# A fifth Strassen pair in two gate branches of a hybrid decoder layer, and norm weights applied per channel

## Chip, cores, metric

The kernel runs on one core of a Trainium2 chip. The time is device time in microseconds (us) of one execution of the program. Engines are called as in the profile: PE is the matrix engine (PEld its weight loads), DVE is VectorE, ACT is ScalarE, POOL is GpSimd, SP is the engine that issues most DMAs.

## The reference, cut to what matters

One decoder layer over 256 positions of 2048 channels. One input projection feeds three mixers (a gated linear recurrence, a windowed attention, a short convolution); each is projected back to 2048 channels, weighed by a sigmoid gate computed from the input, and the sum goes through one output projection and a layer norm.

```python
u = x @ w_in[l]                                   # 2048 -> 16896, all float32
...
o_a = o_a * lax.rsqrt(jnp.mean(jnp.square(o_a), axis=-1, keepdims=True) + RMS_EPS)
o_a = o_a.reshape(bsz, t, HGRN_WIDTH) * hgrn_norm_g[l].astype(jnp.float32)
y_a = (o_a.astype(x.dtype) * jax.nn.silu(a_g)) @ w_proj_hgrn[l]
y_b = (o_b * jax.nn.silu(b_g)) @ w_proj_attn[l]
y_c = (o_c * jax.nn.silu(c_g)) @ w_proj_conv[l]
merged = jax.nn.sigmoid(m_a) * y_a + jax.nn.sigmoid(m_b) * y_b + jax.nn.sigmoid(m_c) * y_c
y = merged @ w_out[l]
x = layer_norm(ALPHA * x + y, ln_g[l], ln_b[l])
```

## The kernel before

Every float32 product is made of three matmuls on two-part numbers: a weight block is split into `hi` (rounded, made by ACT, line 114) and `lo` (the rest, made by DVE, line 115), x likewise, and PE adds x-hi times `hi`, x-lo times `hi` and x-hi times `lo`. Weights come in loads of 1 MB into three `raw` buffers; `hi` and `lo` have four buffers each. `w8` is a pool of twelve 8 KB tiles (`t8`) that everything long-lived shares; `w4` holds smaller tiles of the mixers and is closed before the gates begin, and `mgp` then takes its memory.

First come the input projections, with the mixers cut into small steps (`tasks`) that `pump` strews between the projections' loads; the last of the input projections is the convolution `conv(3)`, whose results are added up by ACT copies `rest` and DVE (lines 191, 192, 541). `sums_of_x`, one of these tasks, loads x again and makes the sums of blocks that the Strassen scheme needs.

Then, for each branch (a, b, c) and each half of the gate's columns, `pair_of_groups` computes 256 rows by 1024 columns of gate from 2048 input channels, and two `gemm` calls do the branch's projection. That makes six gate calls, call 0 (branch a) to call 5 (branch c). A seventh call computes half of the output projection (`w_out2`). Each call goes through eight *pairs of rows*: a pair is 256 input channels, two blocks of 128. A plain pair multiplies 2 x 2 blocks of x with 2 x 2 blocks of weights in 8 products of 3 matmuls. A pair marked in `PAIRS` uses Strassen's scheme in Winograd's form: 7 products, of sums of x (made beforehand) and sums of weights. For these DVE makes four weight sums `w` (lines 696 to 698) out of `raw`, and `w` is split into `hw` (ACT, 2048 columns) and `lw` (DVE); of `raw` itself only three blocks out of four are split. `hw` and `lw` lie in `mgp`, one buffer each, or, for every second marked pair, in `w8`, as far as `spare` says. Marked are pairs 1, 3, 5 and 7.

The eight sums of products gather in eight PSUM banks. `p1`, `p2`, `p6`, `p7` are of the pool `accp`, which the projections use too, so `p6` and `p7` take the banks of the projection just before; `p5`, `p3`, `p4`, `px` are of the pool `bgp`. After a projection DVE evacuates its two banks (lines 749 and 750; line 752 in branch a; 767 with the statistics of line 770 in the output projection).

In which order the products of a marked pair are written is chosen in this line (`whole` needs only `hi` and `lo`, `summed` needs `hw` and `lw`, of `rest` one needs `hi2` and one `hw`):

```python
for n, y in enumerate(whole + summed + rest if raw_first or end else summed + rest[::-1] + whole):
    product(*y, end)
```

The order written in the code is not the order on the engines: a planner sorts each engine's instructions by its own estimate of when operands and buffers are ready, among those ready by the order of writing, and each engine then works through its queue in that fixed order.

The norm weights of branch a (`gn`, 1024 values spread to all partitions) are multiplied into the gate by POOL (line 592); the recurrence's last step transposes its output and splits it with `split_to` (lines 87, 88).

Of the kernel before, what the change touches and what calls it, by code (L numbers as in the profile page):

```python
# [16 lines left out]
P = 128  # L17
T = 256
# [26 lines left out]
PAIRS = (0, 1, 0, 1, 0, 1, 0, 1)  # L45
# [5 lines left out]
def hybrid_kernel(ctx, tc, a, out):  # L51
# [15 lines left out]
    def t8(shape, name, dt=F32):  # L67
        return w8.tile(shape, dt, tag="w8", name=name)
# [131 lines left out]
    def constants():  # L200
# [15 lines left out]
        c["gn"] = const.tile([P, HW], F32, name="gn")  # L216
        nc.sync.dma_start(out=c["gn"], in_=a["hgrn_norm_g"].partition_broadcast(P))
# [67 lines left out]
    def hgrn(hf, fk, q, v, gate):  # L285
# [148 lines left out]
        for i, ps in transpose_pairs([[o[:, t, h * P : h * P + P] for t in range(2)] for h in range(4)], "oaT"):  # L434
            split_to(outs["a"][hf][:, i : i + 2], ps)
            yield
# [112 lines left out]
    def sums_of_x():  # L549

        n = len(pairs)
        xr = rawp.tile([P, n, 2, T], F32, tag="raw", name="xr")
        for i, p in enumerate(pairs):
            nc.sync.dma_start(out=xr[:, i], in_=a["xT"][:, 2 * p : 2 * p + 2])
        sx = t8([P, 4, n, P], "sx")
        block_sums([sx[:, j] for j in range(4)], xr[:, :, 0, :P], xr[:, :, 1, :P], xr[:, :, 0, P:], xr[:, :, 1, P:])
        yield
        for i in range(0, n, 2):
            dst = t8([P, 2, 4, 2, P], "sums", F32R)
            sums.append(dst)  # L560
            for j in range(2):
                split_to(dst[:, j], sx[:, :, i + j])
            yield
# [13 lines left out]
    for hf in range(2):  # L577
# [53 lines left out]
    pairs = [p for p in range(KT // 2) if PAIRS[p]]  # L631
    sums = []
# [10 lines left out]
    msums = []  # L643

    def turn(m, d):
        dst = t8([P, 4, 2, T], "m", F32R)
        ms.append(dst)
        if d % 2 == 0:
            msums.append(t8([P, 2, 4, 2, P], "msums", F32R))
        for i, ps in transpose_pairs([[m[:, t, c * P : c * P + P] for t in range(2)] for c in range(4)], "mT"):  # L650
            split_to(dst[:, i : i + 2], ps)
            if PAIRS[2 * d + i // 2]:
# [4 lines left out]
                split_to(msums[d // 2][:, d % 2], sx)  # L657
            yield

    def pair_of_groups(src, x, sums, raw_first, spare):  # L660
# [18 lines left out]
        final = max(p for p in range(KT // 2) if not PAIRS[p])  # L679
        for p in range(KT // 2):  # L680
# [3 lines left out]
            if not PAIRS[p]:  # L684
# [18 lines left out]
            i = pairs.index(p)  # L703
# [3 lines left out]
            sx = [[sums[i // 2][:, i % 2, j, m] for m in range(2)] for j in range(4)]  # L707
# [214 lines left out]
```

## Time and profile before

| | us |
|---|---|
| median of three runs | 1003.6 (1002.97 to 1003.93) |
| the profiled execution | 1002.37 |
| its span, first to last instruction | 1000.5 |
| PE busy | 984.0 |
| DVE busy | 797.5 |
| ACT busy | 562.3 |
| POOL busy | 32.4 |

A share of busy time is an average over all stages. Matmuls are listed longer than the distance of their starts, since they are pipelined. Times in rows are from the span's start.

### The profile page before, as it was taken

What the parts mean: (1) busy time and instruction counts of PE and PEld (TensorE: products, weight loads), DVE (VectorE), ACT (ScalarE), POOL (GpSimd) and SP (SyncE); (2) the same over time, 40 slices, a digit from 0 to 9 for tenths busy, and PEclk for the clock granted to TensorE, in tenths of its full rate; (3) what the DMA queues carried; (4) which work ended last, traced back from release to release, by engine and by line L of the source; (5) the groups of instructions that cost most, each with busy time, mean ns of one, the idle gap of its engine ahead of it and who ended that gap; (6) DMA issues with size and microseconds to landing.
All of it is one profiled execution on the core that took longest, in us unless ns stands there. A gap on an engine that the chain in (4) does not pass through costs nothing.

```text
span 1000.5 us, 13721 instructions
## 1 busy us (share of the span) xinstructions
PE 984.0 (98%) x5430; PEld 828.5 (83%) x5430; DVE 797.5 (80%) x1000; ACT 562.3 (56%) x735; POOL 32.4 (3%) x32
## 2 busy tenths in 40 slices
PE   8999999999999999999999999999999999999995
PEld 5888888888888888888888888888888888888884
DVE  6557889689955666767778898887989889897997
ACT  5545668557564655645655555555555555564551
POOL 1000100220010000000000000000000000000003
PEclk9999999999999999999999999999999999999998
DMA  8755545444455445544555655555645556548542
GB/s 318 261 174 205 176 161 172 166 171 168 171 179 200 174 163 187 192 169 165 185 197 177 229 190 205 209 210 196 214 180 209 211 193 215 182 171 338 206 168 84
DMA packets 30831, 193.67 MB, mean 194 GB/s; under 512 B 3840, under 2 KB 4640, under 8 KB 8752
## 3 DMA queue, kind: packets, MB, share of 16 engines
q1 hardware_dynamic: 28944, 185.90, 52.4%
q10 hardware_dynamic: 1152, 4.72, 1.2%
q0 software_dynamic: 672, 2.20, 0.7%
q8 instruction: 42, 0.69, 0.3%
q14 instruction: 21, 0.17, 0.0%
HBM read 190.68 MB, written 2.12 MB: 193 GB/s over the span
## 4 chain that ended last, share of the span: by engine, by line
PE 96%; DVE 2%; DMA 1%; SPq 0%; issue 0%; ACT 0%
PE acc L151 25%; PE acc L150 12%; PE p L671 9%; PE p L673 9%; PE p L672 9%; PE acc L145 9%; PE acc L143 9%; PE acc L144 8%; DMA raw<-in_w_rows 1%; PE sc L464 1%; PE acc L153 1%; PE pvb L506 1%; DVE xres L793 1%; DVE xres L791 1%; PE pT L497 1%; PE lev L390 0%
## 5 line engine op out<-in xcount | busy, mean ns | idle before, releaser
L114 ACT CAST hi<-raw 128x1024 fp32r<-128x1024 f32 (+1 forms) x341 | 343.9, 1013 | 317.1 <-PE p L672 107.9
L115 DVE TENSOR_TENSOR lo<-raw,hi 128x1024 fp32r<-128x1024 f32 (+1 forms) x341 | 397.0, 1175 | 111.4 <-ACT hi L114 109.5
L151 PE MATMUL acc<-xs,hi 128*128 128x512 f32 x1056 | 372.0, 397 | 0.0
L150 PE MATMUL acc<-xs,lo 128*128 128x256 f32 x990 | 279.0, 282 | 0.0
L151 PEld LDWEIGHTS acc<-xs,hi 128*128 128x128 f32 x1056 | 197.3, 188 | 44.4 <-issue 1.2
L150 PEld LDWEIGHTS acc<-xs,lo 128*128 128x128 f32 x990 | 186.9, 189 | 3.7 <-issue 1.2
L671 PE MATMUL p<-hi,xs 128*128 128x512 f32 x240 | 93.5, 390 | 0.0
L673 PE MATMUL p<-lo,xs 128*128 128x512 f32 x240 | 93.5, 389 | 0.0
L672 PE MATMUL p<-hi,xs 128*128 128x512 f32 x240 | 93.5, 389 | 0.0
L115 DVE TENSOR_TENSOR lw<-w,hw 128x2048 fp32r<-128x2048 f32 x28 | 64.2, 2293 | 22.3 <-ACT hw L114 20.9
L143 PE MATMUL acc<-hi,xs 128*128 128x512 f32 (+1 forms) x160 | 60.2, 376 | 2.3 <-ACT hi L114 2.3
L145 PE MATMUL acc<-lo,xs 128*128 128x512 f32 (+1 forms) x160 | 59.0, 371 | 0.3 <-DVE lo L115 0.3
L144 PE MATMUL acc<-hi,xs 128*128 128x512 f32 (+1 forms) x160 | 59.0, 369 | 0.0
L114 ACT CAST hw<-w 128x2048 fp32r<-128x2048 f32 x28 | 53.6, 1913 | 9.6 <-DVE w L698 9.5
L673 PEld LDWEIGHTS p<-lo,xs 128*128 128x128 f32 x240 | 45.1, 188 | 9.4
L672 PEld LDWEIGHTS p<-hi,xs 128*128 128x128 f32 x240 | 45.1, 188 | 9.3
L671 PEld LDWEIGHTS p<-hi,xs 128*128 128x128 f32 x240 | 45.1, 188 | 9.3
L191 ACT COPY rest<-acc 128x256 f32<-128x256 f32 x66 | 24.0, 372 | 42.1 <-PE acc L151 41.4
L143 PEld LDWEIGHTS acc<-hi,xs 128*128 128x128 f32 x160 | 30.2, 189 | 10.0 <-ACT hi L114 4.7
L145 PEld LDWEIGHTS acc<-lo,xs 128*128 128x128 f32 x160 | 30.1, 189 | 6.6 <-DVE lo L115 1.6
L696 DVE TENSOR_TENSOR w<-raw 128x1024 f32<-128x1024 f32 x28 | 34.2, 1220 | 0.9 <-DMA raw<-in_w_gate 0.7
L144 PEld LDWEIGHTS acc<-hi,xs 128*128 128x128 f32 x160 | 30.2, 189 | 4.7
(261 smaller groups left out, 1458.6 us busy)
## 6 DMA issues: line engine op xcount, KB each, us to landing
raw<-in_w_cols SPq DMA_DIRECT2D x68, 1024.0 KB, 4.8
raw<-in_w_gate SPq DMA_DIRECT2D x48, 1024.0 KB, 4.8
raw<-in_w_out SPq DMA_DIRECT2D x16, 1024.0 KB, 4.8
raw<-in_w_rows SPq DMA_DIRECT2D x12, 1024.0 KB, 4.8
raw<-in_w_proj_hgrn SPq DMA_DIRECT2D x8, 1024.0 KB, 4.8
raw<-in_w_proj_attn SPq DMA_DIRECT2D x8, 1024.0 KB, 4.8
raw<-in_w_proj_conv SPq DMA_DIRECT2D x8, 1024.0 KB, 4.8
raw<-in_w_rows SPq DMA_DIRECT2D x7, 512.0 KB, 8.7
```

Source lines behind the costliest of these rows:

```text
L114: nc.scalar.copy(out=hi, in_=r)
L115: nc.vector.tensor_sub(out=lo, in0=r, in1=f32(hi))
L143: nc.tensor.matmul(out=acc, lhsT=xk[:, 0, ts], rhs=hi, start=first, stop=False)
L144: nc.tensor.matmul(out=acc, lhsT=xk[:, 1, ts], rhs=hi, start=False, stop=False)
L145: nc.tensor.matmul(out=acc, lhsT=xk[:, 0, ts], rhs=lo, start=False, stop=last)
L150: nc.tensor.matmul(out=acc[:, :T], lhsT=lo, rhs=xk[:, 0], start=False, stop=False)
L151: nc.tensor.matmul(out=acc, lhsT=hi, rhs=xk, start=first, stop=last)
L191: nc.scalar.copy(out=rest[p], in_=acc[p, T:])
L671: nc.tensor.matmul(out=ps, lhsT=x[0], rhs=hi, start=begins, stop=False)
L672: nc.tensor.matmul(out=ps, lhsT=x[1], rhs=hi, start=False, stop=False)
L673: nc.tensor.matmul(out=ps, lhsT=x[0], rhs=lo, start=False, stop=last)
L696: nc.vector.tensor_sub(out=w[:, 0:2], in0=raw[:, 0:1].to_broadcast([P, 2, NC]), in1=raw[:, 1::2])
```

## The change

The marked pairs become 0, 2, 3, 5 and 7 in branches b and c (calls 2 to 5), and 0, 2, 5 and 7 in branch a and in `w_out2`. Pair 0 is thus a Strassen pair in every call. For pair 0, and for all but the last in branch a and `w_out2`, products are written as `rest`, `summed` in reverse, `whole`. The block sums of x are made in three lots (two pairs, two pairs, one pair), their raw sums in `w4`, and the fifth pair's split sums have a tile of their own, `fifth`. `gn` shrinks to one value per channel and partition, and is applied where branch a's output is split after its transposition; the POOL product goes.

```diff
-PAIRS = (0, 1, 0, 1, 0, 1, 0, 1)
+PAIRS, FEWER = (0, 2, 3, 5, 7), (0, 2, 5, 7)
...
-        c["gn"] = const.tile([P, HW], F32, name="gn")
-        nc.sync.dma_start(out=c["gn"], in_=a["hgrn_norm_g"].partition_broadcast(P))
+        c["gn"] = const.tile([P, 8], F32, name="gn")
+        nc.sync.dma_start(out=c["gn"], in_=a["hgrn_norm_g"])
...
-            split_to(outs["a"][hf][:, i : i + 2], ps)
+            for j in range(2):
+                g = C["gn"][:, 4 * hf + i + j : 4 * hf + i + j + 1]
+                dst = outs["a"][hf][:, i + j]
+                nc.scalar.mul(out=dst[:, 0], in_=ps[:, j], mul=g)
+                nc.vector.scalar_tensor_tensor(out=dst[:, 1], in0=ps[:, j], scalar=g, in1=f32(dst[:, 0]),
+                                               op0=ALU.mult, op1=ALU.subtract)
...
-        n = len(pairs)
-        xr = rawp.tile([P, n, 2, T], F32, tag="raw", name="xr")
-        for i, p in enumerate(pairs):
-            nc.sync.dma_start(out=xr[:, i], in_=a["xT"][:, 2 * p : 2 * p + 2])
-        sx = t8([P, 4, n, P], "sx")
-        block_sums([sx[:, j] for j in range(4)], xr[:, :, 0, :P], xr[:, :, 1, :P], xr[:, :, 0, P:], xr[:, :, 1, P:])
-        yield
-        for i in range(0, n, 2):
-            dst = t8([P, 2, 4, 2, P], "sums", F32R)
-            sums.append(dst)
-            for j in range(2):
-                split_to(dst[:, j], sx[:, :, i + j])
+        fifth = const.tile([P, 4, 2, P], F32R, name="fifth")
+        for at in range(0, len(PAIRS), 2):
+            ps = (FEWER + tuple(p for p in PAIRS if p not in FEWER))[at : at + 2]
+            n = len(ps)
+            xr = rawp.tile([P, n, 2, T], F32, tag="raw", name="xr")
+            for i, p in enumerate(ps):
+                nc.sync.dma_start(out=xr[:, i], in_=a["xT"][:, 2 * p : 2 * p + 2])
+            sx = t4([P, 4, n, P], "sx")
+            block_sums([sx[:, j] for j in range(4)], xr[:, :, 0, :P], xr[:, :, 1, :P], xr[:, :, 0, P:], xr[:, :, 1, P:])
+            yield
+            dst = t8([P, n, 4, 2, P], "sums", F32R) if n == 2 else None
+            for i, p in enumerate(ps):
+                sums[p] = dst[:, i] if n == 2 else fifth
+                split_to(sums[p], sx[:, :, i])
             yield
...
-        nc.gpsimd.tensor_mul(out=gate, in0=gate,
-                             in1=C["gn"][:, hf * NC : hf * NC + NC].rearrange("p (o n) -> p o n", o=1)
-                             .to_broadcast([P, 2, NC]))
...
-            for n, y in enumerate(whole + summed + rest if raw_first or end else summed + rest[::-1] + whole):
+            for n, y in enumerate(whole + summed + rest if p and (raw_first or end) else rest + summed[::-1] + whole):
...
-            sg = pair_of_groups(a["w_gate"][2 * n + half], xs, sums, n > 0, 2 if n else 1)
+            sg = pair_of_groups(a["w_gate"][2 * n + half], xs, sums, PAIRS if n else FEWER, n > 0, 2 if n else 1)
...
-    y = pair_of_groups(a["w_out2"][0], ms, msums, False, 0)
+    y = pair_of_groups(a["w_out2"][0], ms, msums, FEWER, False, 0)
```

`turn` makes the sums of the merged rows for the pairs in `FEWER` in the same way as before for the pairs in `PAIRS`.

## Rows read from the trace of the kernel before

**Rows 1.** The page's first section: busy time, share of the span, instructions.

```profile
PE 984.0 (98%) x5430; PEld 828.5 (83%) x5430; DVE 797.5 (80%) x1000; ACT 562.3 (56%) x735; POOL 32.4 (3%) x32
```

**Rows 2.** Waits of PE: engine, line, waited for: us in total, times, longest.

```profile
PE acc L143 <- ACT hi L114: 2.3, 2, 1.3
...
PE acc L145 <- DVE l L115: 0.7, 1, 0.7
PE acc L145 <- DVE lo L115: 0.3, 1, 0.3
```

**Rows 3.** Timeline of PE in call 0: start, duration (us), what [idle before].

```profile
523.22 0.39 PE L671 MATMUL p<-hi,xs 128*128 128x512 f32 x1
...
528.66 0.39 PE L671 MATMUL p<-hw,sums 128*128 128x512 f32 x1
528.89 0.39 PE L672 MATMUL p<-hw,sums 128*128 128x512 f32 x1
529.12 0.39 PE L671 MATMUL p<-hw,sums 128*128 128x512 f32 x1
529.34 0.39 PE L672 MATMUL p<-hw,sums 128*128 128x512 f32 x1
529.57 0.39 PE L671 MATMUL p<-hw,sums 128*128 128x512 f32 x1
529.81 0.73 PE L673 MATMUL p<-lw,sums 128*128 128x512 f32 x2
```

**Rows 4.** Lines by shape, whole run: busy us, mean ns | idle before, releaser.

```profile
L115 DVE TENSOR_TENSOR lo<-raw,hi 128x1024 fp32r<-128x1024 f32 x311 | 378.0, 1222 | 108.4 <-ACT hi L114 106.7
L115 DVE TENSOR_TENSOR lw<-w,hw 128x2048 fp32r<-128x2048 f32 x28 | 64.2, 2293 | 22.3 <-ACT hw L114 20.9 <-PE p L673 1.4
L114 ACT CAST hw<-w 128x2048 fp32r<-128x2048 f32 x28 | 53.6, 1913 | 9.6 <-DVE w L698 9.5
L696 DVE TENSOR_TENSOR w<-raw 128x1024 f32<-128x1024 f32 x28 | 34.2, 1220 | 0.9 <-DMA raw<-in_w_gate 0.7
L698 DVE TENSOR_TENSOR w<-raw,w 128x512 f32<-128x512 f32 x28 | 19.3, 688 | 0.4
```

**Rows 5.** Busy time of each engine in one gate call with its projections (call 3).

```profile
core 0: us, PE busy (x) PEld busy (x) DVE busy (x) ACT busy (x) POOL busy (x), PEclk, DMA share, GB/s
711.00:773.60 62.60, 62.60 (x277) 51.86 (x277) 56.35 (x59) 35.10 (x33) 0.00 (x0) 1.00 0.57 202
```

**Rows 6.** Lines in calls 1 to 5 (586 to 877 us), DVE, then ACT by shape.

```profile
L115 DVE TENSOR_TENSOR lo<-raw,hi 128x1024 fp32r<-128x1024 f32 x113 | 125.8, 1127 | 19.2 <-ACT hi L114 18.4
...
L114 ACT CAST hi<-raw 128x1024 fp32r<-128x1024 f32 x93 | 97.9, 1053 | 111.8 <-PE p L672 72.3 <-PE acc L144 27.3 <-issue 11.0
```

**Rows 7.** Timeline of ACT and DVE around call 0, then DVE before call 4.

```profile
523.07 0.78 ACT L191 COPY rest<-acc 128x256 f32<-128x256 f32 x2 [1.38 <-PE acc L151]
...
524.27 1.92 ACT L114 CAST hw<-w 128x2048 fp32r<-128x2048 f32 x1
...
527.47 2.28 DVE L115 TENSOR_TENSOR lw<-w,hw 128x2048 fp32r<-128x2048 f32 x1
...
771.53 2.29 DVE L115 TENSOR_TENSOR lw<-w,hw 128x2048 fp32r<-128x2048 f32 x1 [0.85 <-ACT hw L114]
```

**Rows 8.** Timeline around the start of the `w_out2` call: ACT, PE, DVE.

```profile
918.30 2.00 ACT L114 CAST hi<-raw 128x1024 fp32r<-128x1024 f32 x2 [2.58 <-DMA raw<-in_w_out]
...
924.40 0.39 PE L671 MATMUL p<-hi,m 128*128 128x512 f32 x1
...
925.46 0.68 DVE L767 SCALAR_TENSOR_TENSOR xres<-xres,acc 128x512 f32<-128x512 f32 x1
...
928.60 0.75 DVE L770 BATCH_NORM_STATS2 stats<-xres 128x6 f32<-128x256 f32 x2
929.26 0.67 DVE L767 SCALAR_TENSOR_TENSOR xres<-xres,acc 128x512 f32<-128x512 f32 x1
```

**Rows 9.** Norm weights on POOL, and the nearest 128x256 form on DVE.

```profile
L592 POOL TENSOR_TENSOR ga<-ga,gn 128x1024 f32<-128x1024 f32 x2 | 6.6, 3318 | 99.8 <-DVE ga L197 99.8
...
L530 DVE SCALAR_TENSOR_TENSOR yc<-hp,cw,yc 128x256 f32<-128x256 f32 x16 | 6.7, 478 | 0.0
```

More of the change, by code (lines that the diff above doesn't have):

```diff
@@ L630, in hybrid_kernel @@
         tasks.append(attn(hf, q, kz, vb, gate))
-    pairs = [p for p in range(KT // 2) if PAIRS[p]]
-    sums = []
+    sums = {}
     tasks.append(sums_of_x())
@@ L641, in hybrid_kernel @@
     ms = []
-    msums = []
+    msums, dsts = {}, []
     def turn(m, d):
@@ L647, in turn @@
         ms.append(dst)
-        if d % 2 == 0:
-            msums.append(t8([P, 2, 4, 2, P], "msums", F32R))
         for i, ps in transpose_pairs([[m[:, t, c * P : c * P + P] for t in range(2)] for c in range(4)], "mT"):
             split_to(dst[:, i : i + 2], ps)
-            if PAIRS[2 * d + i // 2]:
+            p = 2 * d + i // 2
+            if p in FEWER:
+                n = FEWER.index(p)
+                if n % 2 == 0:
+                    dsts.append(t8([P, 2, 4, 2, P], "msums", F32R))
+                msums[p] = dsts[n // 2][:, n % 2]
                 raw = mgp.tile([P, 2, T], F32, tag="u", name="mraw")
@@ L656, in turn, with pair_of_groups @@
                 block_sums([sx[:, j] for j in range(4)], raw[:, 0, :P], raw[:, 1, :P], raw[:, 0, P:], raw[:, 1, P:])
-                split_to(msums[d // 2][:, d % 2], sx)
+                split_to(msums[p], sx)
             yield
-    def pair_of_groups(src, x, sums, raw_first, spare):
+    def pair_of_groups(src, x, sums, taken, raw_first, spare):
         p1, p2, p6, p7 = [accp.tile([P, NC], F32, tag="acc", name=f"p{i}") for i in (1, 2, 6, 7)]
@@ L678, in pair_of_groups @@
         last = KT // 2 - 1
-        final = max(p for p in range(KT // 2) if not PAIRS[p])
+        final = max(p for p in range(KT // 2) if p not in taken)
         for p in range(KT // 2):
@@ L683, in pair_of_groups @@
             flat = raw.rearrange("p s n -> p (s n)")
-            if not PAIRS[p]:
+            if p not in taken:
                 for s in range(2):
@@ L702, in pair_of_groups @@
             split_w(flat[:, 3 * NC :], hi2, lo2)
-            i = pairs.index(p)
+            i = taken.index(p)
             hw, lw = [t8([P, 4, NC], name, F32R) if i % 2 and n < spare else
@@ L706, in pair_of_groups @@
             split_w(w, hw, lw)
-            sx = [[sums[i // 2][:, i % 2, j, m] for m in range(2)] for j in range(4)]
+            sx = [[sums[p][:, j, m] for m in range(2)] for j in range(4)]
             k = 2 * p
@@ L901 @@
         "lb_param": np.ascontiguousarray(i["lb_param"][0].reshape(8, P).T),
-        "hgrn_norm_g": np.ascontiguousarray(i["hgrn_norm_g"][0]),
+        "hgrn_norm_g": np.ascontiguousarray(i["hgrn_norm_g"][0].reshape(8, P).T),
         "attn_sinks": np.ascontiguousarray(i["attn_sinks"][0]),
```

## Prediction

> **What bounds the kernel now.** I read the page's first section, then who waited for whom on the matrix engine, then its timeline, and only then the other engines. The page gives PE 98% busy [rows 1]; a busy share alone proves little, so the second view decides: after the warm-up the matrix engine waited for another engine four times in the whole run, 2.3 + 0.7 + 0.3 = 3.3 us, and none of these is in a gate product (lines 671 to 673) [rows 2]. The timeline shows how tightly it runs: matmuls of 512 columns start 0.227 us apart (529.57 - 528.66 over four steps), although each is listed with 0.39 us because they overlap [rows 3]. So from the end of the start-up to the tail the time is the number of matmuls times 0.227 us. VectorE is the next engine: 56.35 of 62.60 us in the call shown, beside 51.86 us of weight loads [rows 5]. Its idle time there stands before `lo`, ended by ACT's `hi`, and ACT's stands before `hi`, ended by PE [rows 6]: they wait for buffers that PE still reads. They run ahead and are held back.
>
> **Matmuls removed.** A plain pair has 8 products, a Strassen pair 7, each of 3 matmuls. The second and third branch call `pair_of_groups` four times; each trades one plain pair for a Strassen one: 4 x 1 x 3 = 12 matmuls of 512 columns, 12 x 0.227 = **2.72 us** [rows 3]. The first branch and `w_out2` keep four pairs. Nothing else leaves PE. All 12 are on the path, so this is the whole possible gain.
>
> **VectorE and ScalarE work added there.** A Strassen pair costs VectorE `w` 1.22 + 0.69 + 0.69 (line 697 is the twin of 698), `lo` 1.22 and half a one 0.69, `lw` 2.29: 6.80 us; a plain pair two `lo`, 2.44 [rows 4]. That is 4.36 us more for each of the four calls, beside a VectorE that is idle 6.25 us of such a call [rows 5]. It fits with 1 to 2 us over, if the idle time is usable; since it is time in which buffers were full [rows 6], I count it as usable. ScalarE gets about 1.4 us more per call (`hw` 1.91, less half a `hi` of 1.05) and is busy 35.10 of 62.60 [rows 4 to 6]. Cover: PE's own 61.9 us per call. Where the cover is thinnest is the neighbouring pairs 2 and 3. From the call's first matmul to the first use of pair 3's `lw` are 21 + 24 + 21 + 8 = 74 matmuls, 16.8 us; VectorE has in that time the four evacuations (4 x 0.69, taking lines 749 and 750 as long as line 698), one `lo` of pair 1, and two Strassen pairs: 2.8 + 1.2 + 13.6 = 17.6 us. So `lw` comes 0.8 us late by durations. Bounds per call: 0 (what is ready runs first, next part) to 0.8; I take 0.05 per call, near the row that shows no loss [rows 3].
>
> **The first pair becomes a Strassen pair, in all seven calls.** A plain first pair needs only `hi` and `lo`; now it needs `w`, `hw`, `lw`, and VectorE owes the evacuations of the projection before. In the middle calls this is cheap: pair 1's `lw` already runs from 771.53 to 773.82 [rows 7], around the start of its call at 773.6 [rows 5], and pair 0's load lands one slot earlier. The hard place is call 0. There `hw` of today's first Strassen pair (pair 1) stands on ACT's queue behind both `rest` copies of the last convolution (523.07), starts at 524.27, and `lw` runs from 527.47 to 529.75 [rows 7]; PE reads it at 529.81, with 0.06 us to spare [rows 3]. The call starts at 523.22 [rows 3], and the new order (`p3`, then `p4`) asks for `lw` at its sixth matmul, 523.22 + 5 x 0.227 = 524.36. If `lw` came when it comes now, a matrix engine that keeps the written order would stand still 529.75 - 524.36 = **5.4 us**. But the order is not the written one: five matmuls on `hw` stand in front of the first on `lw`, while the code has two [rows 3]. The planner puts what is ready first. Ready without `hw` and `lw` are 3 matmuls of `p3`, 6 of `p1` and `p2`, and of plain pair 1 all but the 6 that add to `p4`, 18: 27 x 0.227 = 6.1 us, and 8 more once `hw` is there. That covers to 529.3 and beyond, so I take 0.1; bounds 0 and 5.4.
>
> **`w_out2`.** The order changes for its pairs too, and pair 0 is Strassen. Its `raw` lands late: ACT waits for it until 918.30, and PE starts the call at 924.40 [rows 8]. Chain: `w` 2.60, `hw` 1.91, `lw` 2.29 [rows 4] give 925.1 (both `lo`, 1.91, fit beside `hw`); needed at 924.40 + 5 x 0.227 = 925.5. Just in time. Behind it on VectorE are the evacuations of the row before: 0.68, two statistics 0.75, 0.68 [rows 8], so until 927.2, while `p7`, which takes the second accumulator's bank, comes at the tenth matmul, 924.40 + 9 x 0.227 = 926.4: **0.8 us** late, 2.0 if one `lo` goes ahead of it. The lower bound is 0, since today VectorE is just as late there (the second evacuation at 929.26 [rows 8]) and PE doesn't wait. I take 0.2, nearer to the row without a wait, because the planner can put the evacuation first.
>
> **Norm weights and sums.** The POOL product (3.32 us, twice) and its 512 KB load go; nobody is recorded as waiting for them. In exchange each of four 128x512 splits becomes two of 128x256, on VectorE 2 x 0.48 for 0.69 [rows 9], four times: 1.1 us, on ScalarE about as much. The sums run in three lots of 2, 2 and 1 pairs: eight additions of 128x256 and four of 128x128 for four of 128x512, by halves of the 0.69 of such an operation [rows 4], with an allowance of 0.07 for each start (0.42 and 0.24, an estimate), 1.6 us more, one split more (0.69), one load of 256 KB more on SP's queue, where the weight loads behind it wait, and three `raw` slots held in turn instead of one. All of it lies beside convolutions, where PE waits for nothing [rows 2]; the gain is 0 for the same reason. Without cover it would be 3.4 us of VectorE time. I take 0, with 0 to 0.5.
>
> **Sum.** -2.72 + 0.2 (four calls) + 0.1 (call 0) + 0.2 (`w_out2`) = -2.2 us. The profiled execution took 1002.37, so it becomes 1000.2; it lies 1.23 below the median of the three runs (1003.6), so the forecast in their terms is **1001.4 us**, 0.22% faster. About 0.2%, 2.0 us, can be told from no change, so the forecast is faster by little: it holds while all new waits stay under 0.7 us.
>
> **Rivals.** *(a) The gain goes into short waits.* `w_out2` 0.8 to 2.0, pairs 2 and 3 up to 0.8 in four calls (3.2), call 0 up to 0.5: 0.8 to 5.7; I take 2.2, since these lie on VectorE one behind the other and rarely all at their worst: 1003.1, no change that can be told. For it: these are the two places where my ledger is late. Against: PE now waits nowhere, though one use has 0.06 us to spare. *(b) Slower: call 0 stands still for `lw`.* Place: the sixth matmul of the call; price 5.4, so -2.7 + 5.4 = +2.7, 1006.3. It decides when PE's queue is kept in the written order, or when more than 4.7 us of the 5.4 stay uncovered. For it: ACT's order in that place [rows 7]. Against: the five matmuls ahead of `lw` [rows 3]. *(c) VectorE is the bound.* If its idle time can't be used, each of four calls grows by 4.36 us and PE's 0.68 are hidden: +17.4, 1021. For it: 90% busy [rows 5]. Against: what ends its idle time [rows 6].
>
> The Trainium skill, "Perfetto Trace Analysis", section "Identifying the Most-Contended Engine", speaks for (c): it takes occupancy as a fair measure for VectorE but not for the matrix engine, where weight loads count. By that rule VectorE (90%) stands before the weight loads (83%), and the time would be (c)'s. The trace differs: PE has no wait in any gate product.
>
> **How the numbers follow.** Forecast 0.46, (a) 0.33, (b) 0.15, (c) 0.06. Range: from the whole gain and a little of the runs' own spread (1003.6 - 2.72 - 0.3 = 1000.6) to the upper part of (a), -2.72 + 4.7 = +2.0, 1005.6. It leaves out (b) and (c), 0.21 in all. Faster by over 0.2%: 0.46; within: 0.33; slower: 0.21.
>
> **What would show it.** PE has 12 instructions fewer (5418), and the starts of the branch b and c calls come 0.68 us closer together each. In call 0 the first matmuls on `hi` of pairs 0 and 1 run before those on `lw`. PE's list of waits stays as it is; a new row of PE or of its weight loads behind `lw` puts the loss into (a) or (b), one behind line 767 into `w_out2`. VectorE's idle time in the four calls falls by about 4 us; if PE's falls behind with it, (c) holds. What makes the prediction wrong is any new PE wait over 0.7 us in sum.

## The result and the profile after

The changed kernel takes **1009.31 us** (median) beside 1003.38 of the kernel before measured with it: a ratio of 1.006, with a 95% interval of 1.0046 to 1.0073. It is slower by 5.9 us where 2.2 us faster was forecast, and it lies above the upper end of the range (1005.6). The profiled execution took 1007.76 us with a span of 1006.0; the one of before took 1002.37 us, span 1000.5. So the two traces differ by 5.5 us.

The page's first section after. Beside [rows 1], PE has 12 instructions fewer and 2.3 us more busy time:

```profile
PE 986.3 (98%) x5418; PEld 826.5 (82%) x5418; DVE 809.9 (81%) x1029; ACT 566.5 (56%) x744; POOL 25.7 (3%) x30
```

PE's waits after (engine, line, waited for: us in total, times, longest). The products now stand in lines 677 to 679; in [rows 2] no wait was in a product, here three are, 3.4 us together:

```profile
PE acc L143 <- ACT hi L114: 2.3, 1, 2.3
PE p L679 <- DVE lw L115: 1.9, 1, 1.9
...
PE p L677 <- ACT hw L114: 0.9, 1, 0.9
PE p L679 <- DVE lo L115: 0.6, 1, 0.6
...
```

The wait for `hi`, here and in every list below, lies in the first 16 us of the program.

Where the 5.5 us lie is read from PE's timeline: the start of the first product of each call, in both traces. The differences, stretch by stretch, for this kernel and all later ones (calls 2 to 5 up to the start of the last call; us against the trace of before; the medians are of unprofiled runs, in brackets the median of the kernel before on the same chip):

| kernel | first 100 matmuls | to call 0 | call 0 | calls 2 to 5 with projections | last call | behind it | median |
|---|---|---|---|---|---|---|---|
| changed | +0.76 | +1.04 | +2.34 | -0.80 | +2.41 | -0.22 | 1009.31 (1003.38) |
| e1_norm | -0.06 | +0.13 | 0.00 | +0.06 | 0.00 | -0.02 | 1004.48 (1003.57) |
| e2_four | +0.13 | +1.36 | +3.90 | +6.86 | 0.00 | +0.52 | 1015.80 (1003.57) |
| e3_five | +1.39 | +1.25 | 0.00 | -1.41 | +0.36 | +0.03 | 1002.92 (1003.57) |
| e4_out | +0.09 | +1.04 | +3.93 | -0.73 | +1.19 | -0.21 | 1008.46 (1003.57) |
| e5_ln | +1.86 | +0.77 | +2.32 | -0.69 | +0.02 | +4.66 | 1011.11 (1003.13) |
| e6_hw | +0.87 | +1.13 | +0.12 | -0.78 | +4.05 | -0.21 | 1006.78 (1003.13) |
| e7_pool | +0.06 | +0.92 | +0.01 | +4.52 | 0.00 | +0.14 | 1007.35 (1003.13) |
| e8_sums | +1.02 | +0.87 | 0.00 | -0.86 | +0.50 | +0.04 | 1003.53 (1003.13) |
| e9_both | +0.12 | +1.22 | +0.12 | -0.77 | +0.33 | -1.11 | 1002.52 (1003.43) |
| e10_leave | +0.21 | +0.80 | 0.00 | -1.39 | 0.00 | -0.09 | 1002.03 (1003.43) |
| e11_add | -0.81 | +0.81 | 0.00 | -1.29 | +1.50 | +0.03 | 1002.47 (1003.43) |
| e12_lo2 | +1.56 | +1.06 | +0.04 | -0.83 | +1.10 | -0.01 | 1003.71 (1003.33) |
| e13_best | +0.98 | +0.62 | +0.05 | -1.34 | 0.00 | -0.52 | 1001.52 (1003.20) |
| e14_last | +0.38 | -0.19 | 0.00 | -0.02 | 0.00 | -0.55 | 1002.23 (1003.20) |

The first row adds up to the 5.53 us. Two places carry most of it, call 0 and the last call, two of the seven whose pair 0 is now a Strassen pair; the four calls that lost 12 matmuls gave 0.80 us, not 2.72, and 1.04 us are lost ahead of call 0. (Where call 0 lost 3.9 us, the waits were the same 2.3 and the clock fell behind them, as the last section shows.) The three stretches by engine (columns as in [rows 5]: us, then busy us of PE, PEld, DVE, ACT, POOL, then the granted clock). Call 0 and the last call hold 180 matmuls each, 40.8 us by the spacing of [rows 3]; both take 43. The middle row answers [rows 5]: 62.33 us for 62.60, VectorE idle 2.7 us instead of 6.25:

```profile
525.02:568.08 43.06, 41.44 (x181) 33.47 (x179) 34.11 (x33) 23.83 (x24) 0.00 (x0) 1.00 0.50 178
714.70:777.03 62.33, 62.33 (x274) 50.97 (x273) 59.64 (x64) 35.85 (x34) 0.00 (x0) 1.00 0.54 195
927.74:970.72 42.98, 41.03 (x180) 33.47 (x179) 38.31 (x40) 23.76 (x24) 0.00 (x0) 1.00 0.59 214
```

**Calls 2 to 5 after.** PE's own list of waits shows nothing here, but that of its weight loads does. In the kernel before, no weight load of these calls waits for `hw` or `lw`; now 16 do (same columns):

```profile
PEld p L679 <- DVE lw L115: 2.1, 9, 0.3
PEld p L677 <- ACT hw L114: 1.6, 7, 0.3
```

What one of them does to PE, in call 3: `hw` ends at 734.51, its weight load can only then run, and the next matmul starts 0.33 us later instead of 0.227:

```profile
734.56 0.19 PEld L677 LDWEIGHTS p<-hw,fifth 128*128 128x128 f32 x1 [0.28 <-ACT hw L114]
```

```profile
734.57 0.50 PE L677 MATMUL p<-hw,fifth 128*128 128x512 f32 x1
734.90 0.40 PE L678 MATMUL p<-hw,fifth 128*128 128x512 f32 x1
```

Fifteen steps of this kind, of 0.25 to 0.34 us, make up 1.2 of the 1.9 us that are missing from the 2.72; the rest lies mostly in steps of 0.23 to 0.24 us.

**Call 0 after.** The timeline of ACT, then of PE (start, duration, engine, line, operation; in square brackets the idle time before it and who ended it):

```profile
524.86 0.79 ACT L191 COPY rest<-acc 128x256 f32<-128x256 f32 x2 [1.38 <-PE acc L151]
525.54 2.00 ACT L114 CAST hi<-raw 128x1024 fp32r<-128x1024 f32 x2
527.44 1.90 ACT L114 CAST hw<-w 128x2048 fp32r<-128x2048 f32 x1
```

```profile
525.02 0.39 PE L677 MATMUL p<-hi,sums 128*128 128x512 f32 x1
...
526.64 0.50 PE L677 MATMUL p<-hi,xs 128*128 128x512 f32 x1
526.98 0.40 PE L678 MATMUL p<-hi,xs 128*128 128x512 f32 x1
528.02 0.49 PE L679 MATMUL p<-lo,xs 128*128 128x512 f32 x1 [0.64 <-DVE lo L115]
529.39 0.50 PE L677 MATMUL p<-hw,xs 128*128 128x512 f32 x1 [0.88 <-ACT hw L114]
```

`hw` runs behind the last `rest` copies and behind two `hi`, 2.58 us after the copies began; in [rows 7] it was 1.20 us. From 525.02 to 529.39 PE ran nine matmuls, 2.0 us of work in 4.4 us.

**The last call after.** VectorE's timeline, then ACT's `hw`, then PE's (PE's call begins at 927.74). Compare [rows 8]:

```profile
921.42 1.23 DVE L702 TENSOR_TENSOR w<-raw 128x1024 f32<-128x1024 f32 x1 [1.17 <-DMA raw<-in_w_out]
922.59 1.23 DVE L115 TENSOR_TENSOR lo<-raw,hi 128x1024 fp32r<-128x1024 f32 x1
923.73 0.69 DVE L703 TENSOR_TENSOR w<-raw,w 128x512 f32<-128x512 f32 x1
924.45 0.69 DVE L704 TENSOR_TENSOR w<-raw,w 128x512 f32<-128x512 f32 x1
925.06 0.68 DVE L115 TENSOR_TENSOR lo<-raw,hi 128x512 fp32r<-128x512 f32 x1
927.50 1.23 DVE L702 TENSOR_TENSOR w<-raw 128x1024 f32<-128x1024 f32 x1 [1.76 <-DMA raw<-in_w_out]
928.65 2.28 DVE L115 TENSOR_TENSOR lw<-w,hw 128x2048 fp32r<-128x2048 f32 x1
930.85 0.68 DVE L773 SCALAR_TENSOR_TENSOR xres<-xres,acc 128x512 f32<-128x512 f32 x1
```

```profile
925.17 1.92 ACT L114 CAST hw<-w 128x2048 fp32r<-128x2048 f32 x1 [2.10 <-DVE w L704]
```

```profile
928.65 0.39 PE L678 MATMUL p<-hw,m 128*128 128x512 f32 x1
930.98 0.50 PE L679 MATMUL p<-lw,m 128*128 128x512 f32 x1 [1.95 <-DVE lw L115]
```

`hw` was done at 927.09, so `lw` could have started then. VectorE stood from 925.7 on for the load of pair 2, whose `w` is planned ahead of this `lw`. Only then came `lw`, at 928.65, 1.56 us later than its data allowed, and PE waited 1.95 us. The evacuation (line 773), which the prediction feared, comes behind all this and costs nothing that shows.

### The profile page after: what moved, and what is told of

The parts are those of the page before. It is cut to its first block, busy times and chain, and to the rows that moved or that the text cites. A ratio compares the mean times of both kernels' runs of the same rounds, so it can differ in the third digit from the quotient of the medians.

```text
span 1006.0 us, 13723 instructions
## 1 busy us (share of the span) xinstructions
PE 986.3 (98%) x5418; PEld 826.5 (82%) x5418; DVE 809.9 (81%) x1029; ACT 566.5 (56%) x744; POOL 25.7 (3%) x30
## 4 chain that ended last, share of the span: by engine, by line
PE 93%; DVE 3%; DMA 1%; ACT 1%; issue 1%; SPq 0%; DVEq 0%
PE acc L151 24%; PE acc L150 12%; PE p L679 9%; PE p L677 9%; PE p L678 9%; PE acc L145 8%; PE acc L143 8%; PE acc L144 8%; PE sc L469 1%; PE acc L153 1%; DMA raw<-in_w_out 1%; DMA raw<-in_w_rows 1%; PE pvb L511 1%; DVE xres L799 1%; PE pT L502 1%
## 5 line engine op out<-in xcount | busy, mean ns | idle before, releaser
L114 ACT CAST hi<-raw 128x1024 fp32r<-128x1024 f32 (+1 forms) x341 | 340.0, 1007 | 305.4 <-PE p L678 94.9
L115 DVE TENSOR_TENSOR lw<-w,hw 128x2048 fp32r<-128x2048 f32 x32 | 73.3, 2290 | 18.8 <-ACT hw L114 18.5
L679 PE MATMUL p<-lo,xs 128*128 128x512 f32 x216 | 84.3, 390 | 0.6 <-DVE lo L115 0.6
L677 PE MATMUL p<-hi,xs 128*128 128x512 f32 x216 | 84.3, 390 | 0.1
L678 PE MATMUL p<-hi,xs 128*128 128x512 f32 x216 | 84.1, 389 | 0.0
L114 ACT CAST hw<-w 128x2048 fp32r<-128x2048 f32 x32 | 61.1, 1910 | 17.2 <-DVE w L704 14.8
L679 PEld LDWEIGHTS p<-lo,xs 128*128 128x128 f32 x216 | 40.6, 188 | 9.5 <-DVE lo L115 1.1
L677 PEld LDWEIGHTS p<-hi,xs 128*128 128x128 f32 x216 | 40.6, 188 | 8.9 <-ACT hi L114 0.5
L678 PEld LDWEIGHTS p<-hi,xs 128*128 128x128 f32 x216 | 40.6, 188 | 8.4
L702 DVE TENSOR_TENSOR w<-raw 128x1024 f32<-128x1024 f32 x32 | 39.1, 1221 | 6.3 <-DMA raw<-in_w_gate 3.2
```

What stands on the lines that cost most here:

```text
L114: nc.scalar.copy(out=hi, in_=r)
L115: nc.vector.tensor_sub(out=lo, in0=r, in1=f32(hi))
L677: nc.tensor.matmul(out=ps, lhsT=x[0], rhs=hi, start=begins, stop=False)
L678: nc.tensor.matmul(out=ps, lhsT=x[1], rhs=hi, start=False, stop=False)
L679: nc.tensor.matmul(out=ps, lhsT=x[0], rhs=lo, start=False, stop=last)
L702: nc.vector.tensor_sub(out=w[:, 0:2], in0=raw[:, 0:1].to_broadcast([P, 2, NC]), in1=raw[:, 1::2])
```

## The experiments

Theory P, the first one: the loss belongs to the places of the first pair, and the fifth pair itself gains. Its rivals: the norm weights (N), or the fifth pair's work on the other engines (F).

**e1_norm**, the norm weights alone on the kernel before:

```diff
...
-            split_to(outs["a"][hf][:, i : i + 2], ps)
+            for j in range(2):
+                g = C["gn"][:, 4 * hf + i + j : 4 * hf + i + j + 1]
+                dst = outs["a"][hf][:, i + j]
+                nc.scalar.mul(out=dst[:, 0], in_=ps[:, j], mul=g)
+                nc.vector.scalar_tensor_tensor(out=dst[:, 1], in0=ps[:, j], scalar=g, in1=f32(dst[:, 0]),
+                                               op0=ALU.mult, op1=ALU.subtract)
...
-        nc.gpsimd.tensor_mul(out=gate, in0=gate,
...
```

> The kernel before with the norm weights alone moved: one weight per channel, applied while the transposed output of branch a is split, and GpSimd's multiplication of the gate gone. Theory P (the loss sits at the places of the first pair, call 0 and the last call): this part costs nothing, 1003.4 us, within 0.5 us. Theory N (the norm weights, which make four short instructions out of two at each transpose, carry the 1.8 us by which the changed kernel is late at the entry of call 0): 1004.7 to 1005.2 us.

Median 1004.48 us, above P's 1003.4 by more than its 0.5 and near N's range; the runs spread widely (1001.37 to 1006.76), and the ratio, 1.0005 (0.9995 to 1.0016), can't be told from no change. The trace decides: call 0 starts 0.07 us later than before, not 1.8, and the last call 0.13. N's mechanism falls, and in the trace this part is free.

**e2_four**, the changed kernel without the fifth pair:

```diff
-PAIRS, FEWER = (0, 2, 3, 5, 7), (0, 2, 5, 7)
+PAIRS, FEWER = (0, 2, 5, 7), (0, 2, 5, 7)
...
```

> The changed kernel without the fifth pair: pairs 0, 2, 5 and 7 in all seven calls, so PE has its 5430 instructions again. Theory P: the waits of 2.3 us in call 0 and of 2.1 us in the last call stay, the lateness of up to 1.8 us before call 0 stays, and the 0.9 us that the b and c calls gained go: 1009 to 1010.5 us. Theory F (the fifth pair's work on VectorE and ScalarE is what delays the rest): the waits go with it and the time returns to that of the kernel before, 1003 to 1004.5 us.

1015.80 us, ratio 1.0118 (1.0102 to 1.0134): slower than either theory gave. F falls, since the fifth pair is gone and the loss is larger. P is right on call 0, but the second place has moved ahead of the last call, into the projection that uses `m`. The waits of PE and VectorE's timeline there:

```profile
PE acc L145 <- DVE lo L115: 4.7, 2, 4.5
...
```

```profile
921.09 1.23 DVE L701 TENSOR_TENSOR w<-raw 128x1024 f32<-128x1024 f32 x1 [9.01 <-DMA raw<-in_w_out]
922.24 1.28 DVE L88 TENSOR_TENSOR m<-mT,m 128x512 fp32r<-128x512 f32 x2
923.43 1.22 DVE L115 TENSOR_TENSOR lo<-raw,hi 128x1024 fp32r<-128x1024 f32 x1
```

VectorE stands 9.01 us for the last call's first `w`, whose load is late, and behind it in the queue are the splits that PE needs at once. It is the mechanism of the changed kernel's last call, in a worse place.

**e3_five**, the fifth pair without the first one:

```diff
-PAIRS, FEWER = (0, 2, 3, 5, 7), (0, 2, 5, 7)
+PAIRS, FEWER = (1, 3, 4, 5, 7), (1, 3, 5, 7)
...
-            for n, y in enumerate(whole + summed + rest if p and (raw_first or end) else rest + summed[::-1] + whole):
+            for n, y in enumerate(whole + summed + rest if raw_first or end else summed + rest[::-1] + whole):
```

> The changed kernel with the fifth pair but without the first one: pairs 1, 3, 4, 5, 7 in the b and c calls, 1, 3, 5, 7 in call 0, call 1 and the last call, products in the order of the kernel before. Theory P: no wait in call 0 nor in the last call; the b and c calls give their 2.72 us less up to 1.8 us of short waits, and up to 1.3 us of lateness ahead of call 0 stays: 1001 to 1003.8 us, PE 5418 instructions. Theory F: the time stays at that of the changed kernel, 1007 to 1010 us.

1002.92 us, ratio 0.9995 (0.9986 to 1.0005). Call 0 loses nothing, the last call 0.36 us. P holds, F is out: the first pair, with the order of products that goes with it, is what made the change slow. This run sets both back and doesn't tell one from the other; e9_both keeps both and loses little in either place, so neither as such is the cost.

**e4_out**, the last call set back to pairs 1, 3, 5, 7 and its old order:

```diff
+LAST = (1, 3, 5, 7)
...
-            if p in FEWER:
-                n = FEWER.index(p)
+            if p in LAST:
+                n = LAST.index(p)
...
-    y = pair_of_groups(a["w_out2"][0], ms, msums, FEWER, False, 0)
+    y = pair_of_groups(a["w_out2"][0], ms, msums, LAST, False, 0)
```

> The changed kernel with the last call (the one on the quads of the output weights) set back to pairs 1, 3, 5, 7 and its old order of products; all else as changed. Theory P: the wait of 2.1 us behind lw in that call goes and the call is 2.4 us shorter: 1006.5 to 1007.5 us beside 1009.3 of the changed kernel. Theory L (the lateness there comes from the loads that stand ahead of it, whichever pair is taken): the wait moves to a hi or lo tile of the same call and the time stays within 0.7 us of the changed kernel's.

1008.46 us, between the two theories: the call loses 1.19 us instead of 2.41, and a wait of 0.9 us for `lw` stays. The choice of the pair with its order is half of it. In this trace the load of pair 1 took 8.9 us from issue to landing, which brought up the loads as the next suspect.

**e5_ln**, the loads of the layer norm's weight and bias moved behind the last call:

```diff
-    lg, lb = t8([P, D], "lg"), t8([P, D], "lbt")
-    nc.scalar.dma_start(out=lg, in_=a["ln_g"].partition_broadcast(P))
-    nc.scalar.dma_start(out=lb, in_=a["ln_b"].partition_broadcast(P))
...
     y = pair_of_groups(a["w_out2"][0], ms, msums, FEWER, False, 0)
+    lg, lb = t8([P, D], "lg"), t8([P, D], "lbt")
+    nc.scalar.dma_start(out=lg, in_=a["ln_g"].partition_broadcast(P))
+    nc.scalar.dma_start(out=lb, in_=a["ln_b"].partition_broadcast(P))
```

> The changed kernel with the loads of the layer norm's weight and bias (2 MB on ScalarE's queue) issued behind the last call instead of ahead of it; the order of VectorE's instructions ahead of that call's lw stays. Theory Q (the wait of 1.9 us behind lw in the last call comes from these loads: the raw tiles of pairs 0 to 2 land 7.1, 7.9 and 7.2 us after their issue, and VectorE stands for w of pair 2 ahead of lw): they land within 5.5 us, the wait falls under 0.7 us, the call takes 41 to 41.6 us instead of 43.0, and the time is 1006.8 to 1008 us beside 1009.3. Theory O (the planned order alone, w of pair 2 and the residual ahead of lw): the wait stays over 1.3 us and the time within 0.7 us of the changed kernel's.

The loads of pairs 0 to 2 in the changed kernel, then here (issues: queue, count, KB each, median us to landing):

```profile
raw<-in_w_out SPq DMA_DIRECT2D x3, 1024.0 KB, 7.2
```

```profile
raw<-in_w_out SPq DMA_DIRECT2D x3, 1024.0 KB, 4.9
```

The wait for `lw` is gone and the call takes its 40.8 us (+0.02): Q holds on the cause, though VectorE still ran pair 2's `w` ahead of `lw`. The forecast time does not: 1011.11 us. The moved loads now travel with those of the last product, of which three take 5.8 to 7.0 us to land where the changed kernel's first three take 4.7 to 4.8. VectorE makes one of the four `l` of that product ahead of the last call's evacuation instead of two, and PE waits for the next:

```profile
PE acc L145 <- DVE l L115: 3.4, 1, 3.4
...
```

```profile
963.92 1.22 DVE L115 TENSOR_TENSOR l<-raw,h 128x1024 fp32r<-128x1024 f32 x1
...
975.51 1.23 DVE L115 TENSOR_TENSOR l<-raw,h 128x1024 fp32r<-128x1024 f32 x1
```

Behind that wait the granted clock was 0.50 for 5.5 us (976.7 to 982.2), which is part of the 4.66 us.

The Trainium skill, "DMA: Bandwidth & Descriptors", section "Issuing engines are not separate DMA queues", says that transfers started by different engines run on the same DMA engines and interleave; the 7.2 us beside the other queue's loads and the 4.9 us without them agree.

**e6_hw**, `hw` of call 0's first pair in a tile of the large pool:

```diff
...
-            hw, lw = [t8([P, 4, NC], name, F32R) if i % 2 and n < spare else
+            hw, lw = [t8([P, 4, NC], name, F32R) if i % 2 and n < spare or first_call and not i and n < 1 else
...
```

> The changed kernel with hw of the first pair of call 0 in a free tile of the large pool (where the odd pairs have theirs) instead of a tile of the pool that takes over the mixers' memory. Theory T (hw is held by that memory, not by its data): ScalarE runs hw ahead of the last two copies of rest, at about 518 us instead of 527.4, PE no longer waits 0.9 us for it, and call 0 loses under 1.4 us instead of 2.3: 1007.5 to 1008.5 us beside 1009.3. Theory E (the first pair asks for too much of ScalarE and VectorE ahead of its call, wherever its tiles lie): the wait moves to lo or lw of the same pair and call 0 loses as much as before, 1009 to 1010 us.

ACT's timeline shows `hw` where theory T put it:

```profile
518.30 1.91 ACT L114 CAST hw<-w 128x2048 fp32r<-128x2048 f32 x1
...
525.07 0.79 ACT L191 COPY rest<-acc 128x256 f32<-128x256 f32 x2 [1.38 <-PE acc L151]
```

Call 0 loses 0.12 us instead of 2.34; T holds, and by more than it gave. The median is 1006.78 us, ratio 1.0031 (1.002 to 1.0041). What kept `hw` back was its tile: the small pool is laid on the memory that the mixers used, and is free only when the last convolution has let it go.

**e7_pool**, on e3_five, the additions into `merged` on GpSimd:

```diff
-                        nc.vector.tensor_add(out=merged[d][:, t], in0=merged[d][:, t], in1=sg[j][:, t])
+                        nc.gpsimd.tensor_add(out=merged[d][:, t], in0=merged[d][:, t], in1=sg[j][:, t])
```

> The fifth pair without the first one (as e3_five), with the additions into merged of the b and c branches on GpSimd instead of VectorE: 16 instructions of 0.68 us off VectorE. Theory V (the fifth pair's gain of 2.72 us is half lost because VectorE is full in these calls, and its products come just in time): the calls 2 to 5 take together 2.3 to 2.8 us less than in the kernel before, and the time is 1.0 to 1.4 us below that of e3_five: 1001.4 to 1002 us. Theory G (GpSimd's additions are too slow or hold VectorE up): the time is that of e3_five or longer, 1002.8 to 1006 us.

1007.35 us, 4.4 above e3_five: G holds. GpSimd's two additions here, and VectorE beside them:

```profile
712.00 5.01 POOL L756 TENSOR_TENSOR merged<-merged,sg 128x512 f32<-128x512 f32 x2 [7.28 <-DVE sg L755]
```

```profile
714.68 1.19 DVE L115 TENSOR_TENSOR lo<-raw,hi 128x512 fp32r<-128x512 f32 x1
715.79 2.31 DVE L702 TENSOR_TENSOR w<-raw 128x1024 f32<-128x1024 f32 x1
```

The half `lo` takes 1.19 us for 0.68 and `w` 2.31 for the 1.22 of [rows 4]. So this run says nothing on theory V; e10_leave was made for that. The Trainium skill, "Perfetto Trace Analysis", section "Optimizing Scalar/DVE Operations", says that GpSimd and VectorE share a port, so moving work between them might not help. This run agrees in the outcome, 4.4 us lost; the port itself no run here shows.

**e8_sums**, on e3_five, the sums of four pairs in one lot again and the fifth's later:

```diff
-        for at in range(0, len(PAIRS), 2):
...
+        n = len(FEWER)
+        xr = rawp.tile([P, n, 2, T], F32, tag="raw", name="xr")
...
+            if n == 0 and half == 1:
+                fifth_sums()
```

> The fifth pair without the first one (as e3_five), with the sums of the four pairs in one lot as in the kernel before, and those of the fifth pair formed inside call 1's stretch, where VectorE has room. Theory S (the sums in three lots cost the 0.6 to 1.1 us by which all kernels with them are late at the entry of call 0): call 0 begins within 0.3 us of the kernel before, run-to-run differences at the start of the program taken off, and the time is 0.6 to 1.1 us below e3_five: 1001.8 to 1002.3 us. Theory R (the lateness is another part of the placement, not the sums): entry and time as e3_five, 1002.6 to 1003.3 us.

Ratio 1.0003 (0.9993 to 1.0013); from the hundredth matmul to call 0 it loses 0.87 us, in the middle of what the kernels that are e3_five up to there lose (0.62 to 1.25 in the table). S is not borne out. The 0.55 us by which its calls 2 to 5 gain less than e3_five's hold a new wait of 0.6 us for `hw` in call 2.

**e9_both**, e6_hw's edit with the two loads issued behind those of the last product:

```diff
...
+    lg, lb = t8([P, D], "lg"), t8([P, D], "lbt")
+    nc.scalar.dma_start(out=lg, in_=a["ln_g"].partition_broadcast(P))
+    nc.scalar.dma_start(out=lb, in_=a["ln_b"].partition_broadcast(P))
     for t, at, n in ((0, 0, NC), (1, 0, T), (1, T, T)):
```

> The changed kernel with both places mended: hw of call 0's first pair in the large pool (as e6_hw) and the loads of the layer norm's weight and bias issued behind the loads of the last product, so that they collide neither with the last call's loads nor with that product's. Theory P (the two places carry the loss): call 0 takes 41 us and the last call under 41.3 us, no wait for hw or lw over 0.7 us is left, and the time is 4 to 5.5 us below the 1009.3 of the changed kernel: 1003.8 to 1005.3 us. Theory M (a loss taken away in one place comes back as a wait in the next): 1006 us or more, with a new wait behind l or hi at the end.

**1002.52 us**, ratio 0.9988 (0.9979 to 0.9997), 6.8 us below the changed kernel, more than the 4 to 5.5 expected. Besides the warm-up's, PE's waits are two rows, both in the first 16 us:

```profile
PE acc L143 <- ACT hi L114: 1.7, 2, 1.5
...
PE acc L145 <- DVE lo L115: 0.3, 1, 0.3
```

Call 0 and the last call lose 0.12 and 0.33 us, and the stretch behind is 1.11 us shorter; 0.7 of that is the wait for `l` of [rows 2], which is gone too. P holds. In call 0 and the last call the change costs time through two things that it does not touch: a tile's memory and the place of two loads.

**e10_leave**, on e3_five, without the additions into `merged` in the b and c branches:

```diff
-                        nc.vector.tensor_add(out=merged[d][:, t], in0=merged[d][:, t], in1=sg[j][:, t])
```

> The fifth pair without the first one (as e3_five), with the additions of branches b and c into merged left out (the output then holds branch a alone): 16 instructions of 0.68 us off VectorE, and nothing put on GpSimd. Theory V (VectorE is full in these calls, its products come just in time, and that takes half of the 2.72 us): the calls 2 to 5 take together 2.4 to 2.8 us less than in the kernel before instead of e3_five's 1.4, and the time is about 1.2 us below e3_five: 1001.2 to 1002 us. Theory W (the lost time lies in the order of the work around pairs, not in VectorE's load): it stays within 0.4 us of e3_five, 1002.5 to 1003.3 us.

The calls 2 to 5 gain 1.39 us, as in e3_five (1.41). One call with its projections, e3_five and then this kernel (columns as in [rows 5]):

```profile
713.39:775.93 62.54, 62.54 (x274) 50.85 (x273) 59.94 (x63) 36.07 (x35) 0.00 (x0) 1.00 0.56 204
```

```profile
711.77:773.97 62.20, 62.20 (x274) 51.01 (x273) 57.81 (x59) 36.18 (x35) 0.00 (x0) 1.00 0.57 203
```

VectorE is relieved of 2.1 us in it. This call is 0.34 us shorter than e3_five's and the next 0.28 longer; over the four nothing comes back. The median (1002.03) is 0.9 us lower, under W's range and at the edge of V's, but the trace has the difference ahead of call 0 and in the last call, not in these. So V falls in this form; W is left, though its time was missed.

**e11_add**, on e3_five, the two additions of a row tile in one:

```diff
-                        nc.vector.tensor_add(out=merged[d][:, t], in0=merged[d][:, t], in1=sg[j][:, t])
+                        if t:
+                            nc.vector.tensor_add(out=merged[d], in0=merged[d], in1=sg[j])
```

> The fifth pair without the first one (as e3_five), with the two additions into merged of each row tile of branches b and c made one of 1024 elements: 1.22 us by the row of that size instead of twice 0.68, so VectorE is relieved of 0.28 us in each call, 1.1 us in the four. Theory V: most of that comes back, 0.5 to 1 us below e3_five: 1002 to 1002.4 us. Theory W: no change, 1002.6 to 1003.3 us.

The calls gain 1.29 us: nothing came back, W again, though the 1002.47 us lie just below its range. Ratio 0.999 (0.9981 to 0.9999); the last call waits 1.0 us for `lw` in this trace.

**e12_lo2**, on e3_five, the work taken off VectorE inside the calls instead:

```diff
+            if len(taken) == 5:
+                lo2 = hi2
+                nc.scalar.copy(out=hi2, in_=flat[:, 3 * NC :])
+            else:
+                lo2 = lop.tile([P, HALF], F32R, tag="lo", name="lo")[:, :NC]
+                split_w(flat[:, 3 * NC :], hi2, lo2)
```

> The fifth pair without the first one (as e3_five), with the lo of each pair's fourth quarter left out in the b and c calls (its third matmul takes hi once more, so the number of matmuls is unchanged and the output is off in its low part): five instructions of 0.68 us, 3.4 us in each call, off VectorE inside the calls themselves. A pair costs VectorE 6.78 us there (w 1.22 and twice 0.68, lo 1.22 and 0.68, lw 2.29), a plain pair of row groups 2.44; five and three are 41.2 us beside 177 matmuls of 0.2265 us, 40.1 us of PE; four and four were 36.9 beside 40.8. Theory L (VectorE is overfull within the call, between its pairs, and can't work it off in the projections): 37.8 us fit again, calls 2 to 5 take together 2.1 to 2.7 us less than in the kernel before instead of 1.4, and the time is 0.7 to 1.3 us below e3_five: 1001.6 to 1002.2 us. Theory W (order of the work around pairs, whatever VectorE's load): the gain of the calls stays at 1.2 to 1.6 us and the time at 1002.4 to 1003.3 us.

Ratio 1.0003 (0.9994 to 1.0013), and the calls gain only 0.83 us: L falls. Calls 2, 4 and 5 gain 0.39 to 0.54 us, 1.36 together, beside 1.39 of the same three in e3_five; call 3 loses 0.53. VectorE's timeline there:

```profile
744.14 1.22 DVE L702 TENSOR_TENSOR w<-raw 128x1024 f32<-128x1024 f32 x1
745.28 1.22 DVE L88 TENSOR_TENSOR oc<-yc,oc 128x1024 fp32r<-128x1024 f32 x1
746.41 0.69 DVE L703 TENSOR_TENSOR w<-raw,w 128x512 f32<-128x512 f32 x1
747.02 1.22 DVE L88 TENSOR_TENSOR oc<-yc,oc 128x1024 fp32r<-128x1024 f32 x1
```

Two splits of the next branch's input, 1.22 us each, stand between the three steps of pair 7's `w`, and PE then waits 0.7 us for `hw` of that pair. VectorE had less to do; the order of its work made the wait all the same.

**e13_best** and **e14_last**: e11_add, and the kernel before, each with the two loads behind those of the last product (the edit of e9_both).

> The fifth pair without the first one and with one addition into merged per row tile (as e11_add), and the loads of the layer norm's weight and bias behind the loads of the last product (as in e9_both). Theory K (the later loads are worth the 0.9 us for which the last product waits for l in the kernel before, and remove e11_add's wait of 1.0 us in the last call; the fifth pair's 1.3 us in the b and c calls are its own): no wait for l, the last call under 41.3 us, and 1.5 to 2.5 us below the kernel before, 0.6 to 1.4 us below e14_last: 1000.9 to 1001.9 us. Theory Z (the fifth pair's gain is eaten by the 0.8 to 1.3 us by which the kernels with the changed sums are late at call 0): within 0.5 us of e14_last, 1002 to 1003 us.

> The kernel before with one thing changed: the loads of the layer norm's weight and bias issued behind the loads of the last product instead of ahead of the last call. Both theories: the wait of 0.7 us for l in the last product goes and nothing else moves: 1002.2 to 1002.9 us, 0.5 to 1.1 us below the kernel before. If it is no faster, the gain of e9_both against the kernel before is that of the fifth pair.

e13_best 1001.52 us, ratio 0.9985 (0.9976 to 0.9994); e14_last 1002.23 us, ratio 0.9991 (0.9982 to 1.0). The later loads alone are worth about 1.0 us, and no wait for `l` is left in either: VectorE makes three of the four `l` ahead of the last call's evacuation instead of two. That order is what changed, not the collision, since the last product's loads take up to 9.0 us to land in e14_last (5.0 before). As e9_both lies only 0.9 us below the kernel before, its gain is no more than the loads': mended in both places, the change itself gives nothing that shows (1002.52 beside 1002.23 us). The fifth pair without the first one adds 0.7 us: inside K's range and above Z's 0.5. What Z feared is there too, 1.34 us gained in its calls and 0.81 lost ahead of call 0 against e14_last. Both kernels before it are beaten, by 1.7 us and, from separate measurements, 7.8.

## Why the prediction was wrong

**What bounds the kernel.** Right as far as it went: PE's count times 0.227 us still sets the time, PE has its 5418 instructions, and the two large losses were waits of PE. But a PE without waits says nothing on how much delay its producers can still bear.

**The first pair in call 0** is one of three steps that failed. 0.1 was taken, 2.34 measured. Rival (b) named the place and the sign, but not the wait: PE stood for `lo` and `hw`, and twenty matmuls ran ahead of the first on `lw`. Two assumptions broke. The 27 ready matmuls were counted from the data; the planned order put nine ahead of `hw`, and even of those one waited for its `lo`. And `hw` was taken to come when pair 1's came; it came later, behind the `rest` copies, although its data were ready: held by its tile (e6_hw). The price of 5.4 for the written order was sound: `lw` ended at 531.66, 5.5 us after its turn in that order.

**`w_out2`** is the second. 0.2 was taken within 0 to 2.0; 2.41 was measured, above the bound. The chain `w`, `hw`, `lw` was added up as if VectorE did nothing else between its links; in the trace a `lo` stands between the parts of `w`, and pair 2's `w` with its 1.76 us of waiting for a load stands ahead of `lw`. The evacuation that was priced in its stead cost nothing. The load's lateness was seen in [rows 8], but not asked for its cause, the two loads on the other queue (e5_ln, e9_both).

**The matmuls removed** and **VectorE's work in the four calls.** All 12 are gone. From one call's start to the next it is 0.49, 0.23, 0.08 and 0.00 us less instead of 0.68 each, and that comes to the 0.80 us; the loss of 0.5 us a call lies inside the bounds of 0 to 0.8, but the 0.05 that was taken is the third step that failed: 0.2 for the four calls, 1.92 measured. (a) had the kind of loss right, short waits from pairs 2 and 3 on, and took 2.2 for all of them. VectorE's idle time fell by 3.6 us in a call, near the 4 forecast. The remainder goes into the 16 waits of weight loads: in calls 3 to 5 `lw` of pair 2 and `hw` and `lw` of pairs 3 and 5 end 0.05 to 0.4 us before PE takes them, where the spare time of such tiles before the change was 3 to 9 us, and each such place costs up to 0.11 us. Why they come so late is settled only in part. It is not VectorE's total load, as (c) had it (e10_leave, e11_add, e12_lo2); in e12_lo2 the order of VectorE's work was seen to do it. A hand-made order was not tried.

The Trainium skill, "Perfetto Trace Analysis", section "Identifying the Most-Contended Engine", would have the engine with the highest occupancy optimized first, here VectorE (96% of call 3 beside 82% for the weight loads). The measurement decides against it: 2.1 us less of VectorE's work in a call returned nothing in e10_leave.

**Norm weights and sums.** The norm weights cost nothing that the trace shows (e1_norm). The sums were taken at 0, within 0 to 0.5. Every kernel with changed sums or pairs is 0.6 to 1.4 us late between the hundredth matmul and call 0, while e1_norm and e14_last are at +0.13 and -0.19; the pieces are too small to place, and e8_sums did not single out the three lots. It stays open.

**Sum.** With the two places mended, e9_both comes to 0.9 us below the kernel before where 2.2 was forecast, and that includes 1.1 us behind the last call that the forecast did not have. So the short waits of calls 2 to 5 (1.95 us lost instead of 0.2) and the lateness ahead of call 0 (1.22) alone would have spent the gain: the first two steps decided that the kernel became slower, the third and the lateness that it could not become faster. Chances of 0.15 for (b) and a range without it were too little for a row of [rows 3] that showed 0.06 us to spare, and no rival added up two places of more than 2 us.

## What to carry to other kernels

When a step is to come first in a stage, follow its whole chain through the queues: what the planner puts between its links, which memory its tiles take over, and which other loads its own load travels with. A use that has 0.06 us to spare in the trace is a price tag, and so is a load that lands late for no reason of its own. Loads that are needed last belong behind those that are needed next, and moved by one place too few they carry the collision to loads that are needed soon (e5_ln against e9_both). And a list of PE's waits is not enough: ask that of its weight loads too.

## What was not expected of the hardware

**The clock after a wait.** In call 0 the changed kernel and e4_out have the same waits (their 2.3 us are two gaps of 0.8 and 1.1 us and a shorter one, at the same matmuls). Just behind them the changed kernel's PE keeps its clock and e4_out's does not (columns as in [rows 5]; the granted clock is the third from the end):

```profile
529.50:533.00 3.50, 3.50 (x16) 2.87 (x17) 2.16 (x1) 1.30 (x1) 0.00 (x0) 1.00 0.70 281
```

```profile
529.00:532.50 3.50, 3.50 (x11) 2.68 (x11) 1.99 (x1) 1.47 (x1) 0.00 (x0) 0.60 0.63 257
```

0.60 is a stretch mostly at 1.2 GHz instead of 2.4, and matmuls then start 0.43 us apart. That is the difference between 2.34 and 3.93 us in call 0. In e6_hw's trace it follows the wait of 2.0 us in the last call, which so lost 4.05 us; the same wait in the changed kernel's trace left the clock at 1.00:

```profile
926.60:930.00 3.40, 1.40 (x6) 0.84 (x6) 3.40 (x4) 1.34 (x2) 0.00 (x0) 1.00 0.38 157
930.00:933.20 3.20, 3.20 (x9) 2.49 (x9) 3.20 (x7) 0.00 (x0) 0.00 (x0) 0.52 0.00 0
```

So a wait of 2 us costs up to twice its length, in some executions and not in others. The four times of the changed kernel, 1007.76, 1007.87, 1010.74 and 1010.80, lie in two groups 3 us apart, with mean granted clocks of 0.995, 0.995, 0.993 and 0.991; that this is the reason is likely, not shown. In e9_both, without these waits, ten runs lie within 2.2 us, but e1_norm's ten, without them too, spread over 5.4.

**The start-up** shows the same two clocks: e3_five and e7_pool run the same work from 11 to 16 us, at a granted clock of 0.66 and 1.00, and are then 1.39 and 0.06 us late. Differences of this size in the first column of the table are not the kernels'.
